# Side work handed out by estimated engine time

## The chip, the cores and the metric

The kernel runs on one core of a Trainium2 chip. A core has five engines with queues of their own: TensorE (matmuls, into the accumulation memory PSUM), VectorE, ScalarE, GpSimd (called POOL in the profile) and SyncE (SP); transfers from and to the chip's memory run on 16 DMA engines, issued from SP's and POOL's queues. The metric is the device time of one execution in microseconds (us). The kernel before takes 2867.68 us, the median of 3 runs (2867.55 to 2868.38).

## The reference

The kernel computes a two-layer encoder trunk in float32 for 512 tokens of 1024 channels. Each layer is

- h = h + 1/2 SwiGLU(RMSNorm(h)), with a hidden width of 2816 (two such feed-forward stages per layer, the second after the mixer);
- h = h + Mixer(RMSNorm(h)).

The mixer projects its input once (`w_in`, 7168 columns) and feeds three branches: a long convolution by FFT with filters that a small network makes (`hyena`, `filter`), a dilated windowed attention with 24 heads and a position bias (`attn`), and a gated linear recurrence run forwards and backwards over time (`rg`). Each branch is projected to 1024 channels, multiplied by a sigmoid gate of the input, and summed; one more projection (`w_out`) ends the mixer. A final RMSNorm gives the output.

## The kernel before, in words

**Main work.** All large products are done on TensorE with every operand split into a high and a low part (`whi` and `wlo` for weights, `xh` and `xl` for inputs), three matmuls of 128 x 512 each for one product (`mm3`, lines 166 to 168). The program is a list, `prog`, of main items. An item with a weight source is a *step*: it uses 512 x 256 weights (or 256 x 512), usually 24 matmuls. There are 470 steps. `run_prog` goes through the list; for step j it issues the weight load of step j + 2 and later as buffers allow (`raw`, two buffers, 512 KB, on SP's queue, line 220), splits it into `whi` (ScalarE, line 238) and `wlo` (VectorE, line 239), each in six buffers of half a step, and then issues the step's matmuls. Two output blocks of 128 channels make a pair (`pair`); a pair takes one, two or more steps, writes two of three PSUM banks, and ends with an evacuation on ScalarE or VectorE (`ev_g`, `ev_u`, `ev_d`, `apart`, `together`, `conv_in`'s `ev`). Feed-forward stages have 44 steps for `wg` and `wu` and 24 for `wd`; the mixer has 100: 8 for the inputs of `rg`, 18 for the first `quad` (queries `q`, keys `k`, values `v` of half the heads), 12 for `conv_in` (the inputs of `hyena`, named `v`, `g0`, `g1`), 12 for a gate and the `rg` projection, 18 for the second `quad`, 12 each for the gates and projections of the other two branches, 8 for `w_out`.

**Side work.** The branches' own computation is written as Python generators, in *portions* that end at each `yield`. `push` puts a generator in one of two lanes (attention and values in lane 1, the rest in lane 0); `pump(n)` issues n portions, taking the lanes in turn, and in a lane always from the oldest generator; `drain(name)` issues portions until a generator is finished, and stands in front of the main item that reads its result. Some portions are empty: a generator that has to wait for a main item yields without issuing anything.

The generators: `filter` has 39 portions, pushed after the first block of the first feed-forward stage and drained six blocks (24 steps) later. `bias` (27 portions, layer 0 only) follows it; 24 of its portions copy a row of the position bias into a temporary buffer on VectorE (line 574) and write it out by DMA on POOL's queue (line 575), 192 KB each for the first head group and 128 KB for the other two. `xn` (4) normalises the mixer's input; `rg` (28) has four gate portions per direction of time, each with 4 matmuls (`psg`, lines 939 and 940) and 7 ScalarE instructions (tanh, exp, square, lines 942 to 946), and then the scans, casts and sums that end in `ych` and `ycl`. `attn` has 25 portions for each half of the heads, `hyena` 45.

**How many portions a step gets.** `rate` is 1; it is 1.35 from the push of `filter` to its drain, and 1.6 from the push of `rg` to the end of the mixer. After each step `credit` grows by `rate`, and its whole part is pumped.

**What sets the order on the engines.** The order in which the code issues is a priority, not yet the order of the queues: the framework's scheduler, at compile time, gives each engine the ready instruction that was issued earliest, and waits where a buffer isn't free. `tc.high_priority(HP)` moves the weight preparation and the evacuations ahead by 20 places. The temporary buffers of 128 x 512 (`tmp`) are six, shared by evacuations and side work. At run time each engine takes its queue in order. So an instruction that waits holds up everything behind it on its engine, and a PSUM bank that is not evacuated holds up TensorE.

Of the kernel before, what the change touches and what calls it, by code (L numbers as in the profile page):

```python
# [19 lines left out]
F32R = mybir.dt.float32r  # L20
# [11 lines left out]
NS = 34  # L32
HP = 20
F0, F1 = 0, 6
RF, RM = 1.35, 1.6
TWO_PI = 2.0 * math.pi


def shape_constants():
# [65 lines left out]
    ("hy_skip", 8), ("rg_conv_w", 16), ("rg_conv_b", 4),  # L105
    ("rg_ba", 8), ("rg_bx", 8), ("rg_lambda", 8), ("b_gate", 24),
]


@with_exitstack  # L110
def trunk(ctx: ExitStack, tc: tile.TileContext, A, out, depth=DEPTH):
    nc = tc.nc
# [17 lines left out]
    def slot(name, dt=F32):  # L130
        return sp.tile([128, 2, 512], dt, tag="sl", name=name)

    def tmp(name, dt=F32):
        return tp.tile([128, 512], dt, tag="t", name=name)
# [10 lines left out]
    def flat(t):  # L145
        return t.rearrange("p a b -> p (a b)")

    def split(hi, lo, src):
        S.copy(hi, src)
        V.tensor_tensor(lo, src, hi.bitcast(F32), ALU.subtract)  # L150
# [28 lines left out]
    def main(fn, src=None, kc=4, cols=256):  # L179
        prog.append((fn, src, kc, cols, 0))  # L180

    def pump(n, lane=None):
        for _ in range(n):
            live = [q for q in lanes if q]
            if lane is not None:
                live = [q for q in live if q is lane]
            while live:
                q = live[turn[0] % len(live)]
                turn[0] += 1
                try:  # L190
                    next(q[0][1])
                    break
                except StopIteration:
                    alive.discard(q[0][0])
                    q.popleft()
                    live = [x for x in live if x]
            else:
                return

    def push(name, gen, lane=0):  # L200
        alive.add(name)
        lanes[lane].append((name, gen))

    def drain(name):
        while name in alive:
            pump(1, next(q for q in lanes if any(n == name for n, _ in q)))

    rate, credit = [1], [0]
    first = [True]

    def run_prog():
        wsteps = [i for i, p in enumerate(prog) if p[1] is not None]
        raws, made = {}, {}
        nxt_raw, nxt_prep = [0], [0]

        def load(j):
            _, src, kc, cols, _ = prog[wsteps[j]]
            raw = rp.tile([128, 4, 256], F32, tag="raw", name="raw")
            if cols == 256:
                nc.sync.dma_start(raw[:, :kc], src.rearrange("(k p) n -> p k n", p=128))  # L220
            else:
                for k in range(kc):
                    dst, rows = raw[:, 2 * k:2 * k + 2], slice(128 * k, 128 * k + 128)
                    nc.sync.dma_start(dst, src[rows].rearrange("p (g c) -> p g c", c=256)
                                      if len(src.shape) == 2 else src[rows])
            raws[j] = raw

        def prep(j, half=None):
            _, src, kc, cols, _ = prog[wsteps[j]]
            if cols == 512:  # L230
                kc *= 2
            raw = raws[j]
            parts = made.setdefault(j, [])
            for k0 in range(0, kc, 2) if half is None else (2 * half,):
                kk = min(2, kc - k0)
                hi = wp.tile([128, 2, 256], F32R, tag="hi", name="whi")
                lo = wp.tile([128, 2, 256], F32R, tag="lo", name="wlo")
                S.copy(hi[:, :kk], raw[:, k0:k0 + kk])  # L238
                V.tensor_tensor(lo[:, :kk], raw[:, k0:k0 + kk], hi.bitcast(F32)[:, :kk], ALU.subtract)  # L239
                if cols == 512:  # L240
                    parts.append((flat(hi), flat(lo)))
                    continue
                for k in range(kk):
                    parts.append((hi[:, k], lo[:, k]))
            if half in (None, 1):
                del raws[j]

        def ahead(n):
            while nxt_raw[0] < min(n, len(wsteps)):
                load(nxt_raw[0])  # L250
                nxt_raw[0] += 1

        def prepare(n):
            while nxt_prep[0] < min(n, len(wsteps)):
                prep(nxt_prep[0])
                nxt_prep[0] += 1

        norm = state["norm"]
        load_x(0)
        ahead(1)  # L260
        load_x(1)
        norm.squares(0)
        norm.half(0, lambda i: i in (1, 2) and prep(0, i - 1))
        nxt_prep[0] = 1
        ahead(2)
        norm.copies()
        norm.half(1)
        prepare(2)
        norm.copies()
        norm.squares(1)  # L270
        norm.end()
        j = 0
        for i, (fn, src, kc, cols, _) in enumerate(prog):
            if src is None:
                fn()
            else:
                with tc.high_priority(HP):
                    ahead(j + 3)
                    prepare(j + 3)
                fn(made.pop(j))  # L280
                j += 1
                credit[0] += rate[0]
                pump(int(credit[0]))
                credit[0] -= int(credit[0])
        pump(10 ** 6)

    def pair(W, X, evac, name):
# [151 lines left out]
    def h(k):  # L439
        return hs[k // 2][:, k % 2]  # L440
# [9 lines left out]
    def load_x(a):  # L450
        if a == 0:
            rows_to_cols(g0, A["ffn1_norm"][0], 8)
        for b in range(4):
            nc.sync.dma_start(xt[b][:, a], A["x"][b::4, a * 512:a * 512 + 512])
# [41 lines left out]
    hyst = [dict() for _ in range(depth)]  # L496

    def ffn(l, which, next_norm):
        wg, wu, wd = A[f"ffn{which}_wg"][l], A[f"ffn{which}_wu"][l], A[f"ffn{which}_wd"][l]
        hid = []  # L500
        X = lambda: state["norm"].x
        for fp in range(DFF // 256):
            st = {}

            def ev_g(c, ps, st=st):
                t = tmp("silu")
                V.tensor_tensor(t, ps, state["norm"].R, ALU.mult)  # L507
                S.activation(t, t, AF.Silu)
                st[c] = t

            def ev_u(c, ps, st=st):
                if c == 0:
                    st["hi"], st["lo"] = slot("hidh", F32R), slot("hidl", F32R)
                t = tmp("up")
                V.tensor_tensor(t, ps, state["norm"].R, ALU.mult)  # L515
                V.tensor_tensor(t, t, st[c], ALU.mult)
                split(st["hi"][:, c], st["lo"][:, c], t)
                hid.append((st["hi"][:, c], st["lo"][:, c]))

            pair(wg[:, fp * 256:(fp + 1) * 256], X, ev_g, "g")  # L520
            pair(wu[:, fp * 256:(fp + 1) * 256], X, ev_u, "u")
            if which == 1 and fp == F0:
                main(lambda: (push("filter", hy_filter(l, hyst[l])), rate.__setitem__(0, RF)))
            if which == 1 and fp == F1:
                main(lambda: (drain("filter"), rate.__setitem__(0, 1)))
                if l == 0:
                    main(lambda: (push("bias", bias_rows()), push("vecs", load_vectors(range(1, depth), 4))))

        def begin():
            state["next"] = next_norm()  # L530

        if next_norm is None:
            down_tokens(wd, hid)
            return
        main(begin)
        for d in range(4):
            def ev_d(c, ps, d=d):
                k = 2 * d + c
                V.scalar_tensor_tensor(h(k), ps, 0.5, h(k), ALU.mult, ALU.add)
                state["next"].add(k, h(k))  # L540

            pair(wd[:, d * 256:(d + 1) * 256], lambda: hid, ev_d, "d")

        def end():
            hid.clear()
            state["next"].end()
            state["norm"] = state["next"]

        main(end)
# [571 lines left out]
    def mixer(l, next_norm):  # L1121
# [50 lines left out]
                pair(W[:, c0 + o + i * 256:c0 + o + i * 256 + 256], X, ev, key)  # L1172
        main(lambda: drain("xn"))
        main(lambda: push("rg", rg(l, srg)))
        main(lambda: rate.__setitem__(0, RM))

        def apart(st, g, c, ps):

# [159 lines left out]
        def end():  # L1338
            state["next"].end()
            state["norm"] = state["next"]  # L1340
            del state["mx"]
            rate[0] = 1

        main(end)


# [81 lines left out]
    for l in range(depth):  # L1428
# [6 lines left out]
        else:  # L1435
            main(lambda: push("ht", to_tokens()))
            ffn(l, 2, None)
    run_prog()


# [33 lines left out]
```

## Time and profile before

| | |
|---|---|
| median of 3 runs | 2867.68 us (2867.55 to 2868.38) |
| the profiled execution, device time | 2868.96 us |
| its span, first to last instruction | 2867.2 us |
| TensorE matmuls busy | 2843.1 us, 99% of the span |
| VectorE busy | 1666.7 us, 58% |
| ScalarE busy | 1200.9 us, 42% |
| GpSimd busy | 172.4 us, 6% |
| mean granted TensorE clock | 0.999 of full speed |

The profile shows one execution. An engine's busy share is an average over stages with different limits. Matmuls are pipelined: the next one starts while one is still being finished, so the busy time of one matmul is longer than the distance between the starts of two. "Idle before, releaser" in a row is how long the engine had nothing running before the instruction, and which instruction's end let it go. The views also give the DMA's time from issue to landing, and TensorE's granted clock in a stretch of time. Names such as `v` or `g` stand for several tiles: `v` is the output of a pair both of `quad` and of `conv_in`.

### The profile page before, as it was taken

How to read it: one execution, taken by the hardware profiler on the slowest of the kernel's cores; microseconds unless marked ns; L12 is line 12 of the kernel's file. 1: busy time of each engine (PE TensorE's matmuls, PEld its weight loads, DVE VectorE, ACT ScalarE, POOL GpSimd, SP SyncE). 2: the span in 40 equal slices, each digit the busy share in tenths (PEclk: the TensorE clock that was granted, in tenths of full speed). 3: DMA queues.
4: the chain of work that ended last, by engine and by line, in shares of the span. 5: the costliest groups of instructions: out<-in, count | busy, mean ns of one | idle time of the engine just before them, and what ended most of it. 6: DMA issues, size and time to landing. Idle time of an engine off the chain costs nothing.

```text
span 2867.2 us, 35629 instructions
## 1 busy us (share of the span) xinstructions
PE 2843.1 (99%) x13379; PEld 2366.2 (83%) x13379; DVE 1666.7 (58%) x3028; ACT 1200.9 (42%) x2101; POOL 172.4 (6%) x321
## 2 busy tenths in 40 slices
PE   9999999999999999999999999999999999999998
PEld 7887888788888888888888888887888888888887
DVE  5785456586675555444377743556757655654533
ACT  5443336844333444333244432477533443433323
POOL 2001110110001000000010000001000110000000
PEclk9999999999999999999999999999999999999999
DMA  4436633232222233332344333333322322333332
GB/s 147 129 112 130 140 115 103 81 122 96 89 93 88 67 126 95 99 100 90 102 119 131 112 92 117 115 96 110 100 89 89 101 81 74 125 94 97 96 103 88
DMA packets 260732, 297.52 MB, mean 104 GB/s; under 512 B 14196, under 2 KB 241632, under 8 KB 260560
## 3 DMA queue, kind: packets, MB, share of 16 engines
q1 hardware_dynamic: 244240, 256.41, 29.2%
q0 software_dynamic: 16160, 38.77, 5.4%
q8 instruction: 105, 1.72, 0.3%
q14 instruction: 67, 0.55, 0.1%
q10 hardware_dynamic: 160, 0.07, 0.0%
HBM read 276.84 MB, written 18.35 MB: 103 GB/s over the span
## 4 chain that ended last, share of the span: by engine, by line
PE 94%; ACT 4%; DVE 1%; issue 0%; DMA 0%; DVEq 0%; ACTq 0%
PE g L166 7%; PE g L168 6%; PE g L167 6%; PE u L166 6%; PE u L168 6%; PE u L167 6%; PE d L167 4%; PE d L168 4%; PE d L166 4%; PE gt L166 3%; PE gt L168 3%; PE gt L167 3%; PE s L1000 2%; PE pj L167 2%; PE pj L168 2%; PE pj L166 1%
## 5 line engine op out<-in xcount | busy, mean ns | idle before, releaser
L239 DVE TENSOR_TENSOR wlo<-raw,whi 128x512 fp32r<-128x512 f32 x928 | 634.4, 689 | 791.2 <-ACT whi L238 780.0
L238 ACT CAST whi<-raw 128x512 fp32r<-128x512 f32 x928 | 572.4, 620 | 1097.8 <-PE u L167 231.5
L166 PE MATMUL u<-xh,whi 128*128 128x512 f32 x704 | 275.0, 391 | 0.0
L167 PE MATMUL u<-xl,whi 128*128 128x512 f32 x704 | 274.5, 390 | 0.0
L168 PE MATMUL u<-xh,wlo 128*128 128x512 f32 x704 | 274.3, 390 | 0.0
L166 PE MATMUL g<-xh,whi 128*128 128x512 f32 x696 | 272.3, 391 | 1.1 <-DVE up L515 1.1
L167 PE MATMUL g<-xl,whi 128*128 128x512 f32 x696 | 271.4, 390 | 0.0
L168 PE MATMUL g<-xh,wlo 128*128 128x512 f32 x696 | 271.2, 390 | 0.0
L167 PE MATMUL d<-hidl,whi 128*128 128x512 f32 x528 | 205.6, 389 | 0.0
L168 PE MATMUL d<-hidh,wlo 128*128 128x512 f32 x528 | 205.6, 389 | 0.0
L166 PE MATMUL d<-hidh,whi 128*128 128x512 f32 x528 | 205.5, 389 | 0.0
L168 PEld LDWEIGHTS u<-xh,wlo 128*128 128x128 f32 x704 | 132.2, 188 | 27.6
L166 PEld LDWEIGHTS u<-xh,whi 128*128 128x128 f32 x704 | 132.2, 188 | 27.2 <-DVE silu L507 0.5
L166 PEld LDWEIGHTS g<-xh,whi 128*128 128x128 f32 x696 | 130.7, 188 | 28.9 <-DVE up L515 1.6
L167 PEld LDWEIGHTS u<-xl,whi 128*128 128x128 f32 x704 | 132.2, 188 | 26.9
L168 PEld LDWEIGHTS g<-xh,wlo 128*128 128x128 f32 x696 | 130.7, 188 | 27.0
L166 PE MATMUL gt<-nh,whi 128*128 128x512 f32 x384 | 152.9, 398 | 0.0
L167 PEld LDWEIGHTS g<-xl,whi 128*128 128x128 f32 x696 | 130.7, 188 | 26.5
L167 PE MATMUL gt<-nl,whi 128*128 128x512 f32 x384 | 149.7, 390 | 0.0
L168 PE MATMUL gt<-nh,wlo 128*128 128x512 f32 x384 | 149.6, 390 | 0.0
L166 PEld LDWEIGHTS d<-hidh,whi 128*128 128x128 f32 x528 | 99.1, 188 | 20.7
L167 PEld LDWEIGHTS d<-hidl,whi 128*128 128x128 f32 x528 | 99.1, 188 | 20.6
(463 smaller groups left out, 5544.1 us busy)
## 6 DMA issues: line engine op xcount, KB each, us to landing
raw<-in_w_in SPq DMA_DIRECT2D x96, 512.0 KB, 3.6
raw<-in_ffn_wg SPq DMA_DIRECT2D x88, 512.0 KB, 3.7
raw<-in_ffn_wu SPq DMA_DIRECT2D x88, 512.0 KB, 3.7
raw<-in_ffn_wd SPq DMA_DIRECT2D x60, 512.0 KB, 3.4
raw<-in_w_gate SPq DMA_DIRECT2D x48, 512.0 KB, 3.6
raw<-in_ffn_wd SPq DMA_DIRECT2D x56, 256.0 KB, 2.7
raw<-in_w_in SPq DMA_DIRECT2D x32, 256.0 KB, 3.0
raw<-in_w_out SPq DMA_DIRECT2D x16, 512.0 KB, 3.4
```

The costliest lines, as they stand in the source:

```text
L166: T.matmul(ps, lh, rh, start=first, stop=False)
L167: T.matmul(ps, lh, rl, start=False, stop=False)
L168: T.matmul(ps, ll, rh, start=False, stop=last)
L238: S.copy(hi[:, :kk], raw[:, k0:k0 + kk])
L239: V.tensor_tensor(lo[:, :kk], raw[:, k0:k0 + kk], hi.bitcast(F32)[:, :kk], ALU.subtract)
L1000: T.matmul(ps, q[g][c][:, hh % 2, qt], k[g][:, c, kt], start=True, stop=True)
```

## The change

`rate` and `credit` go, with the constants `RF` and `RM` and the three places that set the rate. In their place `estimate` gives a price in us to each instruction of ScalarE, VectorE and TensorE from its type and its number of elements per partition; transfers, GpSimd and everything else have none. After each step `pace` prices all that was issued since the last step (`count`). What ScalarE and VectorE were given beyond TensorE's time of the same stretch is kept as `owed`, never below zero. Then at most two portions (`LANE`) are issued, and none once `owed` plus what was issued since for either engine stands above 3.0 us (`AHEAD`). The portions issued are priced with the next step. Drains are as before.

```diff
-RF, RM = 1.35, 1.6
+AHEAD, LANE = 3.0, 2
...
+def estimate(i):
+
+    if not i.outs:
+        return None, 0.0
+    n = math.prod(c for _, c in i.outs[0].ap[1:])
+    if i.engine == mybir.EngineType.Activation:
+        return 0, 0.2 + 0.85e-3 * n
+    if i.engine == mybir.EngineType.DVE:
+        return 1, {"InstReciprocal": 6.5e-3, "InstTensorTensorScan": 2.4e-3}.get(type(i).__name__, 1.05e-3) * n + 0.15
+    if i.engine == mybir.EngineType.PE:
+        return 2, 0.013 + 0.417e-3 * n if i.ins[1].dtype == F32R else 1.7e-3 * n
+    return None, 0.0
...
-    rate, credit = [1], [0]
+    owed, given, seen = [0.0, 0.0], [0.0, 0.0, 0.0], [0]
+
+    def count():
+        todo = nc.cur_bb.bb.instructions
+        for i in todo[seen[0]:]:
+            e, t = estimate(i)
+            if e is not None:
+                given[e] += t
+        seen[0] = len(todo)
+
+    def pace():
+
+        count()
+        for e in range(2):
+            owed[e] = max(owed[e] + given[e] - given[2], 0.0)
+        given[:] = 0.0, 0.0, 0.0
+        for _ in range(LANE):
+            if max(owed[e] + given[e] for e in range(2)) > AHEAD:
+                break
+            pump(1)
+            count()
...
-                credit[0] += rate[0]
-                pump(int(credit[0]))
-                credit[0] -= int(credit[0])
+                pace()
...
-                main(lambda: (push("filter", hy_filter(l, hyst[l])), rate.__setitem__(0, RF)))
+                main(lambda: push("filter", hy_filter(l, hyst[l])))
...
-                main(lambda: (drain("filter"), rate.__setitem__(0, 1)))
+                main(lambda: drain("filter"))
...
-        main(lambda: rate.__setitem__(0, RM))
...
-            rate[0] = 1
```

## Rows read from the trace of the kernel before

**Rows 1.** The page: busy us (share of the span) and instructions of TensorE.
```profile
PE 2843.1 (99%) x13379; PEld 2366.2 (83%) x13379; DVE 1666.7 (58%) x3028; ACT 1200.9 (42%) x2101; POOL 172.4 (6%) x321
```
**Rows 2.** TensorE's waits: waiting line, releaser, us in total, times, longest.
```profile
PE v L166 <- ACT k L1200: 5.4, 2, 2.7
PE k L166 <- ACT qz L1190: 1.6, 2, 0.8
PE s L1000 <- DVE mst L1004: 1.5, 1, 1.5
PE psg L939 <- ACT ti L943: 1.3, 4, 0.5
...
PE g L166 <- DVE up L515: 1.1, 1, 1.1
...
PE hps L680 <- ACT wo L669: 0.4, 1, 0.4
```
**Rows 3.** TensorE in order of time, layer 0: start, duration, instruction, idle before and releaser.
```profile
553.95 0.39 PE L166 MATMUL k<-nh,whi 128*128 128x512 f32 x1
554.17 0.39 PE L167 MATMUL k<-nl,whi 128*128 128x512 f32 x1
555.34 0.50 PE L166 MATMUL k<-nh,whi 128*128 128x512 f32 x1 [0.78 <-ACT qz L1190]
...
573.66 0.50 PE L166 MATMUL v<-nh,whi 128*128 128x512 f32 x1 [2.69 <-ACT k L1200]
```
**Rows 4.** The same view in layer 1; seven rows alike are left out between.
```profile
1992.76 0.80 PE L166 MATMUL v<-nh,whi 128*128 128x512 f32 x1 [2.71 <-ACT k L1200]
...
1996.21 0.39 PE L168 MATMUL v<-nh,wlo 128*128 128x512 f32 x1
```
**Rows 5.** Windows: length; PE, PEld, DVE, ACT, POOL busy (count); granted clock; DMA share; GB/s.
```profile
540.00:570.00 30.00, 28.67 (x126) 23.20 (x125) 13.79 (x20) 28.89 (x44) 2.70 (x5) 1.00 0.24 66
570.00:600.00 30.00, 25.83 (x130) 21.51 (x129) 29.65 (x90) 12.84 (x18) 7.98 (x15) 1.00 0.54 176
...
1990.00:1995.00 5.00, 2.29 (x6) 1.82 (x6) 5.00 (x7) 3.10 (x4) 2.64 (x5) 0.76 0.62 164
```
**Rows 6.** ScalarE in order of time: a gate portion, and the queue at 568.
```profile
538.26 0.68 ACT L942 ACTIVATE tr<-psg,vec 64x512 f32<-64x512 f32 x1
...
543.55 0.67 ACT L942 ACTIVATE tr<-psg,vec 64x512 f32<-64x512 f32 x1
...
567.91 1.28 ACT L859 ACT_TABLE_LOAD   x1
...
570.98 2.14 ACT L149 CAST ych<-gx 128x512 fp32r<-128x512 f32 x2 [1.57 <-DVE gx L967]
573.00 1.08 ACT L1200 COPY k<-k 128x512 f32<-128x512 f32 x2
```
**Rows 7.** The page's costliest groups: the split of a weight on VectorE and ScalarE.
```profile
L239 DVE TENSOR_TENSOR wlo<-raw,whi 128x512 fp32r<-128x512 f32 x928 | 634.4, 689 | 791.2 <-ACT whi L238 780.0
L238 ACT CAST whi<-raw 128x512 fp32r<-128x512 f32 x928 | 572.4, 620 | 1097.8 <-PE u L167 231.5
```
**Rows 8.** Line 858, the first instruction of `rg`: durations, first and last start.
```profile
L858 ACT ACTIVATE rgs<-vec x2: 208/208/209, 52.7 to 567.7; 128x8 f32<-128x8 f32 x2
```
**Rows 9.** DMA issues by stretch (60 to 200, 215 to 260, 260 to 310): KB, us to landing.
```profile
raw<-in_ffn_wg SPq DMA_DIRECT2D x12, 512.0 KB, 3.8
...
raw<-in_ffn_wg SPq DMA_DIRECT2D x4, 512.0 KB, 10.5
dbias<-row POOLq DMA_DIRECT2D x7, 192.0 KB, 9.8
...
raw<-in_ffn_wd SPq DMA_DIRECT2D x7, 512.0 KB, 5.8
```
**Rows 10.** ScalarE and TensorE's weight loads in order of time, layer 0, during the bias rows.
```profile
263.27 1.14 ACT L238 CAST whi<-raw 128x512 fp32r<-128x512 f32 x2 [8.38 <-DMA raw<-in_ffn_wg]
...
264.82 0.19 PEld L166 LDWEIGHTS g<-xh,whi 128*128 128x128 f32 x1 [0.43 <-ACT whi L238]
```

## The prediction

> **What bounds the kernel now.** I read the engine table first: TensorE is busy 2843.1 of 2867.2 us [rows 1]. So the change can only win what TensorE loses, and the next view is its list of waits. Apart from start and end it is short: 5.4 us on a copy of k, 1.6 on a copy of q, 1.5 on a row maximum, 1.3 on a tanh [rows 2]. Releasers are ScalarE or VectorE each time, and all four belong to the stage in which the side program `rg` runs beside the first `quad` and `conv_in`. A wait costs more than its idle time, because a matmul's 0.39 us overlaps the next: 553.95 and 554.17 stand 0.22 apart, 554.17 and 555.34 stand 1.17 apart, so 0.95 is lost where 0.78 is shown [rows 3]. I add 0.17 per wait: tanh 1.3 + 4 x 0.17 = 2.0; q 1.6 + 2 x 0.17 = 1.9; k 5.4 + 2 x 0.17 = 5.7; maximum 1.5 + 0.17 = 1.7. After the second wait on k the eight matmuls from 1992.76 to 1996.21 take 3.45 us instead of 8 x 0.22 = 1.8, and the granted clock of that stretch is 0.76 [rows 4, 5]: 1.65 more. The stage loses 13.0 us in both layers together. That is the pot.
>
> Who is late there is seen in the windows: from 540 to 570 us ScalarE is busy 28.89 of 30 us, from 570 to 600 VectorE 29.65 of 30 [rows 5]. ScalarE runs the gate portions of `rg` back to back. One of them lasts from 538.26 to 543.55, 5.3 us with one cast of a weight in it, so 4.8 alone [rows 6]. The wait on k has a second part: the copies at 573.00 stand in ScalarE's queue behind two casts that waited 1.57 us for VectorE, and these behind a table load of 1.28 [rows 6].
>
> **The change, part by part.** Computation, tiles and instructions stay; only the step after which a portion is issued moves. A step is 24 matmuls, 24 x 0.2265 = 5.44 us by the new price (24 x 0.22 = 5.3 by [rows 3]). Its own ScalarE work is two casts (620 ns each), VectorE's two subtractions (689 each) [rows 7]; the new prices for them, 0.635 and 0.688, fit.
>
> *Gate portions.* One is 7 ScalarE instructions of 512 elements, 7 x 0.635 = 4.4 us by the new price, 4.8 by [rows 6]. At 1.6 portions a step every second step or so issues two: 8.9 + 1.3 of casts + 1.3 of two copies = 11.4 us of ScalarE against 5.44 + 4 x 2 x 0.2265 = 7.3 of TensorE, 4 us behind at once. Laying all portions out step by step at these prices, ScalarE's lag reaches 6.5 us. By the new rule the account stands above 3 after one gate portion, so a step issues one: 5.7 to 8.3 us against 6.3, and the lag peaks at 1.9. With the 4.8 of the trace and a table load of 1.28 it may come to some 4. A PSUM bank is wanted again one step, 5.4 us, after its last matmul, so this hides. The waits on tanh and q, 3.9 us, go.
>
> *Tail of `rg`.* Its scans and casts are spread: the last portion comes some six steps later. In the eight steps in which they then meet `conv_in` and the first scores, VectorE is asked for 50 us by the new prices while TensorE has 54. The k copies are issued before these casts and no longer stand behind them, but VectorE has little to spare, and the same kind of wait can appear on a `conv_in` bank. Between nothing and all of 5.7 + 1.65 + 1.7 = 9.05, I take two thirds, 6.0, because the head-of-queue cause goes and the load stays.
>
> *Filter.* It may now run at up to two portions a step. Drained at the end are 6 portions in layer 0 instead of 12, and 6 as before in layer 1. The list of waits names 0.4 us there [rows 2]; 0, between -0.5 and +0.5.
>
> *`xn`.* Two portions at once instead of one make VectorE 5.5 us late by the prices instead of 2.7, about the slack of a bank. Before, the layout has it 7.8 late in the `hyena` stage, and none of the waits of [rows 2] lies there; 0, at most +1.
>
> *`hyena` and attention.* `hyena` is left with three portions (one empty) instead of one when it is drained, right before the projection that needs its result. If nothing fills in, that projection waits for two VectorE instructions, a cast and a subtraction: 3 x 0.69 + 0.62 = 2.7 us a layer [rows 7]; if gate matmuls fill in, as now, nothing. Between 0 and 5.4 for both, I take 0.8, near the present state. The attention drains change by one to three portions, whose readers come later: 0.
>
> *Bias rows.* This is what the new price does not see. A bias portion costs 0.4 to 0.6 us on VectorE by its price, so two are issued per step instead of one; but each also writes 128 or 192 KB by DMA on POOL's queue, and that is priced at nothing. At one per step the writes of 192 KB took 9.8 us to land, and the weight loads beside them 10.5 instead of 3.8 [rows 9]. A cast waited 8.38 us for such a load, and TensorE's weight load 0.43 for its cast [rows 10]: the lead of the weights was used up; a wait of 1.1 on `up` lies there too [rows 2]. The row copies also hold some of the six temporary buffers that the evacuations use, and VectorE's queue is in order. The number of rows does not change, only their density. From below: the two waits may vanish, -0.43 - 1.1 - 2 x 0.17 = -1.9. From above, rival C. I take +1.0, near the present state.
>
> The Trainium skill (DMA: Bandwidth & Descriptors, "Queues, rings and completion order") says that a DMA engine takes turns between its queues packet by packet. The trace agrees as far as it goes, 10.5 against 3.8 us [rows 9]. By that rule twice the rows beside a load delay it by up to twice 6.7 us, to 17; by the spacing of the rows alone nothing changes until the lead is gone.
>
> Sum: -3.9 - 6.0 + 0.8 + 1.0 = -8.1. The profiled execution took 2868.96 us (1.76 around its span), so 2860.9; the median of the runs shown lies 1.3 below it: 2859.6.
>
> **Rivals.** *A, as summed:* 2859.6. If all 13.0 go at no cost, 2854.7; if a third of the 9.05 goes and the costs double, -3.9 - 3.0 + 3.6 = -3.3, 2864.4.
>
> *B, the waits only move.* Queues are not in the order of issue: the first instruction of `rg`, priced among the mixer's work, runs at 52.7 us, and that of layer 1 at 567.7 [rows 8]. The order is made at compile time from readiness, so a portion issued late may stand where it stood. Then k and maximum waits return on other banks and only the 3.9 goes, less the 1.8 of costs: -2.1, 2865.6. For it: 50 of 54 us of VectorE. Against: the lag of ScalarE is halved at the least, and a portion cannot run before it is issued with a better place than the copies of its step.
>
> *C, the bias rows starve TensorE.* The place is layer 0's first feed-forward stage, after the filter. With two load buffers a step's weights cost half of landing time plus two casts and a subtraction pair, (L + 2.4) / 2. It decides from L = 8.4 us, where this passes 5.4. If doubled density brings L to 14 over the 13 steps of the rows, (14 + 2.4) / 2 = 8.2, that is 2.8 x 13 = 36 less the lead of two steps, 10.8: +25, so 2859.6 - 1.0 + 25 = 2884. With L = 12 it is +12.6, 2871; slower by the bound begins at L = 12.4. For it: the stretch is at its limit now. Against: beside the 128 KB rows, two thirds of all, the loads landed in 5.8 us [rows 9], and the 192 KB rows would be past in five steps, 5 x 2.8 - 10.8 = +3.
>
> *D, the change does not do what it says:* the account could hold side work back until the drains. The layout speaks against it (drains of 6, 0, 5, 3 and 1 portions against 12, 0, 4, 1 and 4); the lost time would be about what it is now, 2867.7.
>
> **Chances and range.** Within 0.2%, 5.7 us either way, a measurement here cannot tell a change from none: 2862.0 to 2873.4. A 0.60, of which 0.54 below 2862.0; B 0.20; D 0.04; C 0.16, nearly all of it slower. So faster 0.54, same 0.30, slower 0.16. A's own range is 2854.7 to 2864.4; with B, D and the near end of C, 2853 to 2871.
>
> **What would show it.** Right: waits on tanh and q gone from TensorE's list, waits on k at most 2 us in all, ScalarE below 27 of 30 us in every window of the stage, no stretch at half clock in layer 1. Wrong: waits on `conv_in` banks of the old size (B); weight loads landing above 9 us through ten steps and TensorE waiting for casts between 220 and 300 us (C); a wait above 2 us before the `hyena` projection.

## The result: 28.4 us slower

The changed kernel takes 2896.08 us (median of 4 runs, 2894.36 to 2896.57), the kernel before 2867.67 beside it: ratio 1.0097 [1.0083, 1.0111]. The forecast was 2859.6 with a range of 2853 to 2871. Wrong sign, and outside the range.

The page after has TensorE longer busy with the same 13379 instructions; the other engines do the same work in the same time as in [rows 1]. Nothing was added, TensorE is held up.

```profile
PE 2854.2 (99%) x13379; PEld 2371.6 (82%) x13379; DVE 1666.0 (58%) x3028; ACT 1199.4 (41%) x2101; POOL 172.5 (6%) x321
```

TensorE's waits after, to read against [rows 2] (waiting line, releaser, us in total, times, longest):

```profile
PE g L180 <- DVE silu L539: 6.6, 1, 6.6
PE s L1032 <- DVE mst L1036: 5.2, 3, 2.5
PE psg L972 <- DVE rgwl L164: 5.2, 2, 2.6
PE d L180 <- DVE silu L539: 3.8, 1, 3.8
PE g L180 <- DVE up L547: 2.4, 2, 1.4
...
PE v L180 <- DVE v L1333: 1.9, 2, 1.2
```

The waits on tanh, q and k are gone, as forecast. Others stand in their place, and every releaser is now VectorE. Two kinds are there: `silu` and `up` belong to a feed-forward stage, `rgwl`, `mst` and `v` to the mixers.

Where the time went is read from the starts of the same matmul in both traces: the first `d` of layer 0, the first `rx` and the first `wo` of each mixer. First before, then after.

```profile
288.63 0.39 PE L166 MATMUL d<-hidh,whi 128*128 128x512 f32 x1
408.91 0.39 PE L166 MATMUL rx<-xh,whi 128*128 128x512 f32 x1
...
1034.37 0.39 PE L166 MATMUL wo<-mgh,whi 128*128 128x512 f32 x1
...
1827.40 0.39 PE L166 MATMUL rx<-xh,whi 128*128 128x512 f32 x1
...
2451.88 0.39 PE L166 MATMUL wo<-mgh,whi 128*128 128x512 f32 x1
```
```profile
303.36 0.77 PE L180 MATMUL d<-hidh,whi 128*128 128x512 f32 x1 [3.80 <-DVE silu L539]
426.11 0.39 PE L180 MATMUL rx<-xh,whi 128*128 128x512 f32 x1
...
1056.66 0.39 PE L180 MATMUL wo<-mgh,whi 128*128 128x512 f32 x1
...
1851.11 0.39 PE L180 MATMUL rx<-xh,whi 128*128 128x512 f32 x1
...
2479.09 0.39 PE L180 MATMUL wo<-mgh,whi 128*128 128x512 f32 x1
```

The differences are +14.7, +17.2, +22.3, +23.7 and +27.2 us. So layer 0's first feed-forward stage loses 17.2, layer 0's mixer 5.1, the stretch with the second filter 1.4, layer 1's mixer 3.5. Up to the end of the first filter, at 219 us, the two traces differ by 0.9: nearly all of the 17.2 falls beside the bias rows.

The DMA issues of 215 to 260 and 260 to 310 us (KB each, median us from issue to landing) answer to [rows 9]:

```profile
raw<-in_ffn_wg SPq DMA_DIRECT2D x4, 512.0 KB, 12.2
dbias<-row POOLq DMA_DIRECT2D x8, 192.0 KB, 9.3
...
raw<-in_ffn_wd SPq DMA_DIRECT2D x5, 512.0 KB, 8.0
dbias<-row POOLq DMA_DIRECT2D x12, 128.0 KB, 9.5
```

The weight loads land later than before, 12.2 against 10.5 and 8.0 against 5.8 us. One such load, followed to TensorE (start, duration, instruction, idle before and releaser):

```profile
270.70 1.14 ACT L272 CAST whi<-raw 128x512 fp32r<-128x512 f32 x2 [10.72 <-DMA raw<-in_ffn_wg]
271.35 2.66 DVE L273 TENSOR_TENSOR wlo<-raw,whi 128x512 fp32r<-128x512 f32 x4 [12.04 <-ACT whi L272]
...
273.92 0.69 DVE L539 TENSOR_TENSOR silu<-g,R 128x512 f32<-128x512 f32 x1
...
274.75 0.77 PE L180 MATMUL g<-xh,whi 128*128 128x512 f32 x1 [6.57 <-DVE silu L539]
```

The wait names `silu`, but `silu` is not slow. It stands in VectorE's queue behind four subtractions, these wait for ScalarE's cast, and the cast waits 10.72 us for the load. TensorE's last matmul ended at 268.2; it stands until `silu` has freed the next bank. The stall also costs behind its end: the two windows after 270 show the granted clock below full speed, 0.58 meaning that most of the first ran at the lower level, 1.2 GHz (length, PE busy, clock, DMA share, GB/s).

```profile
270.00:276.00 6.00, 1.25 (x3) 0.58 0.44 139
276.00:282.00 6.00, 5.86 (x22) 0.85 1.05 131
```

The row writes reach TensorE on a second path too:

```profile
282.18 0.69 DVE L547 TENSOR_TENSOR up<-u,R 128x512 f32<-128x512 f32 x1 [6.78 <-DMA dbias<-row]
```

Right behind `silu`, from 274.52, VectorE copies four rows into temporary buffers, and their writes hold these until they have landed. `up` needs such a buffer and waits for a write, 6.8 us here and 6.9 once more at 311 us. Behind the first of these TensorE stands 1.1 us, behind the second not at all; `silu` costs it 10.4.

### The profile page after: what moved, and what is told of

Read it like the earlier page. It is cut to its first block, busy times and chain, and to the rows that moved or that the text cites. A ratio compares the mean times of both kernels' runs of the same rounds, so it can differ in the third digit from the quotient of the medians.

```text
span 2894.4 us, 35654 instructions
## 1 busy us (share of the span) xinstructions
PE 2854.2 (99%) x13379; PEld 2371.6 (82%) x13379; DVE 1666.0 (58%) x3028; ACT 1199.4 (41%) x2101; POOL 172.5 (6%) x321
## 4 chain that ended last, share of the span: by engine, by line
PE 90%; issue 4%; ACT 3%; DVE 3%; DMA 1%; POOL 0%; DVEq 0%; ACTq 0%; POOLq 0%
PE g L180 6%; PE g L182 6%; PE g L181 6%; PE u L180 5%; PE u L181 5%; PE u L182 5%; PE d L181 4%; PE d L180 4%; PE d L182 4%; PE gt L182 3%; PE gt L181 3%; PE gt L180 3%; PE s L1032 1%; PE k L182 1%; PE k L181 1%
```

## Experiments

Times are medians; ratios are to the kernel before in the same job, at 2868.0 to 2868.3 us.

### The bias rows: how dense may they be?

**One portion a step while they last** (e1). The change with

```diff
-        for _ in range(LANE):
+        for _ in range(1 if "bias" in alive else LANE):
```

> The changed kernel, but one portion a step for as long as the bias rows are among the side work; all else stays paced by the account. Theory (the bias rows at two a step cost what TensorE loses between 219 and 308 us, 16.3 us): 2896.1 - 16 = 2880, between 2878 and 2883. Rival (the loss of that stretch comes from something else that moved with them, such as the end of the filter): 2892 or more.

Measured 2878.37 us, 1.0037 [1.0024, 1.0050]: 17.7 less than the change. The theory holds, somewhat above its size. The first `d` starts at 286.74, 1.9 us earlier than before.

**Two portions a step in the kernel before** (e5).

```diff
-                credit[0] += rate[0]
+                credit[0] += 2 if "bias" in alive else rate[0]
```

> The kernel before with one thing changed: two portions a step while the bias rows are among the side work. Theory (density of the bias rows alone): 2867.7 + 16 = 2884, between 2880 and 2887. Rival (the old fixed rates elsewhere keep enough in hand, and the loss needs the other moves too): 2872 or less.

Measured 2902.87, 1.0123 [1.0109, 1.0137]: +34.9. The rows alone slow the old kernel too, and by twice what I expected. The trace shows part of the reason: the loads are later than in the change (rows below), and the path by the buffers has grown, `up` waits 17.0 us for row writes and TensorE 7.4 us for `up`. That in the change the account can hold a portion back is a likely further reason, not tested.

**Without the copies on VectorE** (e6). The change, each write reading the table itself:

```diff
-                row = tmp("row")[0:8, 0:w]
-                V.tensor_copy(row, mk[0:8, cs])
-                nc.gpsimd.dma_start(wide[:, r0:r0 + 16], row.unsqueeze(1).to_broadcast([8, 16, w]))
+                nc.gpsimd.dma_start(wide[:, r0:r0 + 16], mk[0:8, cs].unsqueeze(1).to_broadcast([8, 16, w]))
```

> The changed kernel without the 24 VectorE copies of the bias rows: each write to DRAM reads the finished table itself, so the eight writes of a group can be issued at once. Fewer VectorE instructions and no temporary buffers held, but the writes are denser still. Theory 1 (the writes delay the weight loads): no better than the change, 2896 to 2915. Rival (the copies stand in VectorE's queue and hold the temporary buffers of the evacuations): the 16 us go, 2880, between 2878 and 2885.

Measured 2915.1, 1.0164 [1.0150, 1.0178]: 19 us worse than the change although VectorE has 24 instructions less and no temporary buffer is held. So the writes alone suffice for the loss. What the buffers add in the change isn't settled by this run, because its writes are denser: 192 KB land in 23.0 us here.

**Writes of half the size** (e14). The change with 48 portions of 8 rows:

```diff
-            for r0 in range(0, 128, 16):
+            for r0 in range(0, 128, 8):
-                nc.gpsimd.dma_start(wide[:, r0:r0 + 16], row.unsqueeze(1).to_broadcast([8, 16, w]))
+                nc.gpsimd.dma_start(wide[:, r0:r0 + 8], row.unsqueeze(1).to_broadcast([8, 8, w]))
```

> The changed kernel with the bias rows cut in twice as many portions: 48 writes of 8 rows instead of 24 of 16, still as many portions a step as the account allows, so a step writes half the bytes and the VectorE copies and the buffers they hold stay as dense as in the change, for twice as long. Theory (bytes written a step delay the weight loads): about the loss at one full portion a step, 2880, between 2876 and 2884. Rival (the copies and their place in VectorE's queue): 2896 or more.

Measured 2880.47, 1.0042 [1.0030, 1.0055]. Twice the copies and the same bytes in all, and nearly all of the loss is gone. By the DMA view, in part shown below, the stretch from 215 to 310 us holds 30 writes of 2.4 MB here (16 x 96 + 14 x 64 KB), 23 of 3.5 MB in the change and 14 of 2.3 MB in e1. So the loss goes with the bytes, not with the number of writes or copies. A smaller write also frees its buffer sooner, after 5.8 us instead of 9.3; this run doesn't separate the two.

The four traces beside each other, DMA issues of 215 to 310 us: e1, e14, e5 and e6.

```profile
raw<-in_ffn_wg SPq DMA_DIRECT2D x4, 512.0 KB, 3.9
dbias<-row POOLq DMA_DIRECT2D x8, 192.0 KB, 9.2
dbias<-row POOLq DMA_DIRECT2D x6, 128.0 KB, 7.0
```
```profile
raw<-in_ffn_wg SPq DMA_DIRECT2D x4, 512.0 KB, 5.5
dbias<-row POOLq DMA_DIRECT2D x16, 96.0 KB, 5.8
```
```profile
raw<-in_ffn_wg SPq DMA_DIRECT2D x4, 512.0 KB, 21.6
dbias<-row POOLq DMA_DIRECT2D x15, 128.0 KB, 9.9
dbias<-row POOLq DMA_DIRECT2D x8, 192.0 KB, 12.6
```
```profile
raw<-in_ffn_wg SPq DMA_DIRECT2D x4, 512.0 KB, 22.5
dbias<-mk POOLq DMA_DIRECT2D x16, 128.0 KB, 17.4
dbias<-mk POOLq DMA_DIRECT2D x8, 192.0 KB, 23.0
```

These kernels have different mixers, so the loss beside the rows is read from the first `rx`, at 408.9 us before: it comes 0.1 us later in e1, 0.0 in e14, 17.2 in the change, 33.7 in e5 and 34.9 in e6, where `wg` lands in 3.9, 5.5, 12.2, 21.6 and 22.5 us. Late loads and lost time run together. But the 5.4 us of a step is no limit: the kernel before has 10.5 us there [rows 9], and a cast waited 8.4 us for a load [rows 10], at hardly any loss; in e1 one waited 9.8 us. In the change two waited 10.7 and 8.7 us. Where the lead of the weights is used up isn't shown more closely than that.

### The mixers: the account where a gain was forecast

**The account in the mixers alone** (e2). The kernel before, with `estimate`, `count` and `pace` of the change, and

```diff
-                credit[0] += rate[0]
-                pump(int(credit[0]))
-                credit[0] -= int(credit[0])
+                if rate[0] == RM:
+                    pace()
+                else:
+                    ...
+                    credit[0] += rate[0]
+                    pump(int(credit[0]))
+                    credit[0] -= int(credit[0])
```

> The kernel before with the account of the change in the two mixer stages only; the fixed rates stay in the feed-forward stages, the bias rows at one a step. Theory (the account itself costs the mixers 5.1 + 3.5 us): 2867.7 + 8.6 = 2876, between 2873 and 2879. Rival (the mixers lose only because they start from another state after the bias rows): 2868, between 2866 and 2870. My forecast of these stages was a gain of 9: 2859.

Measured 2877.92, 1.0033 [1.0021, 1.0045]: +9.9. The theory holds; the two parts, 17.7 and 9.9, make 27.6 of the 28.4 us.

What happens there in the change, layer 0, VectorE in order of time:

```profile
553.40 2.34 DVE L994 TENSOR_TENSOR_SCAN qq<-aa,gx 128x512 f32<-128x512 f32 x2
555.66 1.20 DVE L164 TENSOR_TENSOR rgwl<-rgw,rgwh 128x1024 fp32r<-128x1024 f32 x1
...
589.10 2.36 DVE L992 TENSOR_TENSOR gx<-gx,qq 128x1024 f32<-128x1024 f32 x2 [2.08 <-ACT qq L991]
...
601.50 0.43 DVE L1036 CUSTOM_DVE_ANT_0 p<-s,bias 128x256 f32<-128x256 f32 x1
```

And TensorE, waiting for the second of these rows and for the score maxima that begin with the last:

```profile
556.91 0.73 PE L972 MATMUL psg<-xcs,rgwl 128*128 128x512 f32 x2 [2.62 <-DVE rgwl L164]
...
602.43 1.19 PE L1032 MATMUL s<-k,qz 128*128 128x128 f32 x4 [2.46 <-DVE mst L1036]
```

The split of the second direction's gate weights stands behind the first direction's scans, and the first score maxima behind the tail of `rg`, which VectorE works off without a gap from 589.10 to 601.50.

The split stood behind the scans in the kernel before too (530.75 us, the last scan from 529.62), and nothing waited for it. What changed is the time left for it, from the last gate matmul of the first direction to the first of the second. First before, then after:

```profile
507.56 0.39 PE L940 MATMUL psg<-xcs,rgwl 128*128 128x512 f32 x1
535.88 0.39 PE L939 MATMUL psg<-xcs,rgwh 128*128 128x512 f32 x1
```
```profile
537.56 0.39 PE L972 MATMUL psg<-xcs,rgwl 128*128 128x512 f32 x1
553.67 0.61 PE L971 MATMUL psg<-xcs,rgwh 128*128 128x512 f32 x2
```

That is 28.3 us before and 16.1 after. The gates are spread, over 22 us instead of 15; what has to run between the two directions (the rest of the last gate portion, the square roots, the scans, the split) is not, and in the change it takes until 556.86, 19.3 us.

ScalarE and VectorE over the same two windows as in [rows 5], 17 us later:

```profile
557.00:587.00 30.00, 30.00 (x126) 24.62 (x127) 11.52 (x19) 26.97 (x43) 2.70 (x5) 0.94 0.28 82
587.00:617.00 30.00, 26.82 (x114) 22.07 (x113) 25.48 (x62) 15.17 (x21) 5.33 (x10) 0.89 0.29 91
```

VectorE has more idle time than before in both, 18.5 and 4.5 us against 16.2 and 0.4. It is not short of time; it gets its work late and in bursts.

**The split earlier** (e7), on e1; the second direction then takes `nxt`.

```diff
...
             if d == 0:
                 raw = gates(1)
+                nxt = slot("rgwh", F32R), slot("rgwl", F32R)
+                split(*nxt, raw)
+                yield
```

> The run with one bias portion a step (2878.4), and in rg the gate weights of the second direction are split before the scans of the first, not behind them. Theory (TensorE waits for that split because VectorE takes the scans first): the two waits of 2.6 us go with the slow matmuls behind them, 2878.4 - 2 x (2.8 + 1.6) = 2869.6, between 2867 and 2872. Rival (VectorE is full there whatever the order, and another wait takes the place): 2876 to 2880.

Measured 2874.49, 1.0023 [1.0014, 1.0032]: 3.9 less than e1, under half of what I expected and between the ranges of theory and rival. The waits on `rgwl` are gone, those on the maxima went from 5.2 to 7.1:

```profile
PE s L1038 <- DVE mst L1042: 7.1, 3, 3.4
```

**Limit of 6 us** (e10), on e1.

```diff
-AHEAD, LANE = 3.0, 2
+AHEAD, LANE = 6.0, 2
```

> The run with one bias portion a step, and the account may stand at 6 us instead of 3 before it holds back. Theory (one gate portion a step leaves VectorE idle between 540 and 570 us and pushes the tail of rg into the first scores): the waits for the score maximum fall from 5.2 us to below 2, those for k or tanh come back in part, 2878.4 - 5 = 2873, between 2870 and 2876. Rival (the waits hang on the order of VectorE's queue, not on when the portions are issued): 2877 to 2880, score waits unchanged.

Measured 2873.31, 1.0018 [1.0009, 1.0027]. As expected: the maxima leave the list, k comes back.

```profile
PE v L180 <- ACT k L1231: 7.0, 2, 3.5
PE psg L972 <- DVE rgwl L164: 2.6, 2, 1.3
```

**Limit and split together** (e17).

> The run with the account's limit at 6 us (2873.3), with the early split of the second direction's gate weights added. Theory (the two edits act on different waits: the split on the 2.6 us left for it, the limit on the score maxima): 2873.3 - 2.6 - 2 x 0.17 - about 0.5 = 2870, between 2868 and 2872. Rival (VectorE is full, the wait moves): 2873 to 2876.

Measured 2874.58, 1.0022 [1.0013, 1.0031]: no gain over either, in the rival's range. A miss; the maxima are back, and k is at 3.1.

```profile
PE s L1038 <- DVE mst L1042: 7.5, 2, 3.8
```

**No limit** (e11), on e1, with `AHEAD` at 1e9.

> The run with one bias portion a step, and no account at all: two portions at every other step. Theory (the tail of rg is early, ScalarE is behind with the gates): no waits for the score maximum, waits for k and tanh larger than before the change (over 7 us), 2868 to 2876. Rival (the account is what keeps the filter and the mixers from much worse): 2882 or more.

Measured 2880.59, 1.0046 [1.0033, 1.0059]: outside the theory's range, no better than e1. With the gates unpaced the waits are on `rgwl` again (4.8) and on a late weight split (4.4); k is at 1.8, not above 7. (The expectation describes the pace wrongly: without a limit two portions go out at every step.)

**k on VectorE** (e20 on the kernel before, e21 on e17). While `rg` is alive, the first quad's copies of k go to VectorE.

```diff
-                S.copy(t, ps)
+                copy(t, ps)
```
with `copy = S.copy if "hyena" in alive or "rg" not in alive else V.tensor_copy`.

> The kernel before, no account, but the copies of k of the first quad run on VectorE instead of ScalarE. Theory (what TensorE lost there was ScalarE's queue, busy 14.8 of 15 us with gates, whatever the pace): the waits on k of 5.4 us and the half-clock stretch go, 2867.7 - 5.7 - 1.7 = 2860, between 2859 and 2864. Rival (from 570 us VectorE is as full as ScalarE was before, and the same wait returns with VectorE's name): 2866 to 2870.

> The account at 6 us, one bias portion a step, early split, and the first quad's copies of k on VectorE. Theory (ScalarE's queue is what is left, 7.0 us of waits on k): about 2870 - 7 = 2863, between 2861 and 2867. Rival (VectorE is late in its place): 2868 to 2874.

Measured 2870.12, 1.0007 [0.9998, 1.0016], and 2869.33, 1.0005 [0.9996, 1.0014]. For e20 the rival was right: the wait came back under VectorE's name, here of e20:

```profile
PE v L166 <- DVE k L1201: 4.8, 2, 2.7
```

In e21 it did so too: the waits on k are 6.5 us there, behind VectorE. The 5.3 us that e21 wins on e17 go with the score maxima, 1.8 us instead of 7.5. It lies in the rival's range and ends level with the kernel before.

**Less ScalarE work** (e24 on the kernel before, e25 on e1). The second tanh and the square of each gate portion are left out, and the gate's value is not computed:

```diff
-                S.activation(tr, tr, AF.Tanh, bias=p4[:, i:i + 1], scale=p4[:, i:i + 1])
-                S.activation(q_, a, AF.Square)
-                V.scalar_tensor_tensor(q_, q_, 1.0, tr, ALU.add, ALU.mult)
+                V.scalar_tensor_tensor(q_, a, 1.0, a, ALU.add, ALU.mult)
```

> The kernel before, fixed rates, with the second tanh and the square left out of each gate portion (the gate's value is not computed): five ScalarE instructions instead of seven, 16 fewer in a layer, 10 us. Theory (ScalarE's load holds the stage): waits on tanh, q and k fall from 8.3 to below 2 us, 2868.2 - 8 = 2860, between 2858 and 2863. Rival (the order of the queues): waits on k stay above 4 us, 2864 to 2868.

> The account of the change, one bias portion a step (2878.4), with the same two ScalarE instructions left out of each gate portion. Theory 1 (load): the account issues more portions a step, the tail of rg is early, and the waits on the second gate weights and the score maxima go: 2878.4 - 14 = 2864, between 2860 and 2868. Rival (order: VectorE's queue holds scans ahead of what TensorE wants, whatever ScalarE does): waits on gate weights and maxima above 6 us together, 2873 to 2878.

Measured 2869.26, 1.0003 [0.9994, 1.0012], and 2861.54, 0.9976 [0.9966, 0.9985]. At the fixed rate 10 us less of ScalarE a layer win nothing, and the time lies above both ranges: waits move from tanh and q to the maxima. Under the account the same cut wins 16.8 us, as theory 1 had it, and `rgwl` and the maxima leave the list. First e24, then e25:

```profile
PE v L166 <- ACT k L1198: 5.3, 2, 3.7
PE s L998 <- DVE mst L1002: 3.3, 1, 3.3
```
```profile
PE v L180 <- DVE v L1331: 1.1, 2, 0.6
```

Theory 1's reason, more portions a step, is not what happened to the gates. In the first direction of layer 0 their matmuls start at 498.69, 505.31, 511.66 and 518.80 us in e1 and at 499.13, 505.71, 512.05 and 519.20 in e25, and the second direction's at 536.92 and 536.83. What differs is ScalarE: it begins the square roots, with a table load, at 528.34 in e1 and at 523.61 in e25, and those of the second direction at 568.26 and 560.43.

So neither theory holds alone. Load is not all, or e24 had won. Order is not all, or e25 had kept its waits. The account's spacing is good where ScalarE follows it, and bad where ScalarE, with seven instructions a portion, falls behind and releases the tail in bursts.

### A better version?

**Half-size rows in the kernel before**: e22 with k on VectorE and one portion a step; e23 without, at one and a half a step, the load of layer 1's vectors issued ahead of the rows.

> The kernel before with the copies of k on VectorE and the bias rows in 48 writes of 8 rows, one a step. Theory (half the bytes a step delay no weight load, and the waits of 1.1 and 0.4 us beside the rows go): 1 to 2 us below the run with the copies of k alone. Rival (twice as many steps beside rows cost as much as they save): the same as that run within 1 us.

> The kernel before with the bias rows in 48 writes of 8 rows, one and a half portions a step while they last, and the load of layer 1's vectors ahead of them and not behind, so that neither is drained in a burst at the mixer. Theory (what cost 15 us before was the burst at the drain; fewer bytes a step beside the weight loads win what the run of 48 writes won before its drain): 2868.2 - 2 = 2866, between 2864 and 2867.5. Rival (no room to win there): 2867.5 to 2871.

Measured 2883.97, 1.0054 [1.0042, 1.0067], and 2866.91, 0.9995 [0.9986, 1.0004]. e22 is a miss: its 48 portions were not done when the mixer drained them (bias writes are issued from 410 to 427 us), and the vectors behind them were loaded with TensorE waiting.

```profile
PE vps L421 <- DMA vraw<-in_rg_conv_b: 11.1, 1, 11.1
```

e23 takes that wait away and is 1.3 us below the kernel before, which its interval doesn't tell from none. No version that computes the reference is measurably faster than the kernel before.

## Why the prediction was wrong

**Bias rows: the step that failed most.** "I take +1.0, near the present state"; measured 17.7 (e1). Rival C had the place, the chain (late load, late cast) and the size: it gave +12.6 for loads of 12 us, they took 12.2. That the size fits is partly luck: C had every load of 13 steps at 12 us, and `wu` and `wd` took 6.8 and 8.0. I gave it 0.16 on two arguments, and both failed. "Beside the 128 KB rows ... the loads landed in 5.8 us" was read at one row a step, which is just what the change alters: at up to two, 8.0. "The 192 KB rows would be past in five steps" priced a steady deficit; the trace has single stalls of 6.6 and 3.8 us with slow matmuls behind them, the second beside the 128 KB rows. I had written that the price doesn't see the writes and that the stretch was at its limit; then the nearest row was the wrong end to take. A quantity that the change doubles can't be priced at its present value.

On the Trainium skill's rule (DMA: Bandwidth & Descriptors, "Queues, rings and completion order"), the queues taking turns packet by packet: the runs agree in direction, more write bytes a step make the loads later (3.9, 12.2, 22.5 us). My estimate from it, up to 17, is no upper end: e5 shows 21.6 at two portions a step.

**Gate portions: -3.9, right in the waits, wrong in the reason.** Waits on tanh and q are gone. But ScalarE was to be below 27 of 30 us in every window of the stage; it is at 26.97 in the window shown and at 28.36 from 516 to 546 us. Its lag was held against the next use of a PSUM bank ("so this hides"). What it delayed was the chain of square roots, scans and split between the two directions, and that had no term in the sum.

**Tail of `rg`: -6.0, failed.** The waits on k went, as forecast. But "VectorE has little to spare" was a sum over eight steps, and the place was wrong: no `conv_in` bank, but the scans ahead of the split of the gate weights, 2.6 us a layer, and the tail ahead of the first score maxima, 2.5 with 1.2 on `v`. These and the slow matmuls behind them (clock 0.94 and 0.89) outweigh what was saved (in layer 1 the clock is 0.78 from 2030 to 2035 us, where no slow stretch was to be): in all the mixers lost 9.9 where I had -9.9 + 0.8. The layout saw how many instructions meet in a step; it didn't see that VectorE takes what is ready first, that portions issued one by one become ready together once ScalarE is behind, and that TensorE then waits for the whole burst.

**B** was right that the waits move, wrong on where and on the price: it had -2.1.

**Filter: 0, right in layer 0** (0.9 late at its end); layer 1's stretch lost 1.4. **`xn`, `hyena`, attention**: apart from the maxima and `v`, counted above, no wait over 1 us on the list belongs to them; the forecast 0.8 is not seen.

**Chances.** The term of 1.0 and rival C stood on the same rows, and the range took in C's near end only. C's 2871 to 2884 still rests on the gain in the mixers: with their loss of 9.9 in place of a gain of 9.1 it becomes 2890 to 2903, which holds the time. The two errors added up, and no rival had both.

What stays open: how much of the mixers' 9.9 falls to each of the two bursts, since each edit moved the other, and how much of the 17.7 to the buffers that the writes hold. Loads into three buffers instead of two, and attention held back until `rg` is done, would have told more; they were not tried.

## What to carry to other kernels

A pacer that prices only engines' busy time will speed up just the portions whose cost is elsewhere: give a portion that writes memory a price in bytes, or a ceiling of its own. Nor does busy time price a chain: spread what stands at its front, and less time is left for what must run behind it. A wait is read back through the queue of the engine it names: `silu` was blocked by a load two engines away. And pacing by issue holds only as long as the slowest engine follows; where it can't, first cut its work, then pace.

## What was not expected of the hardware

The 192 KB row writes land in nearly the same time at one and at up to two a step, 9.2 and 9.3 us, while the 512 KB loads beside them go from 3.9 to 12.2. The smaller writes do give way: 128 KB take 7.0 us in e1 and 9.5 in the change. At 30 writes of half the size in the stretch instead of 23 whole ones the loads are back at 5.5.

And the 10.5 us of [rows 9], which I took for the price of one row a step, is no steady price: e1 has one a step too, and 3.9. The rhythm differs. In the kernel before four rows are copied between 224 and 234 us; in e1 they go in pairs 10 to 13 us apart. That this is the reason isn't shown. The filter's last two writes are not: in the kernel before they had landed by 222 us, ahead of the first row at 225.
